# A decoder layer on one core: the pool branch behind the u products, the samples' attention in steps between gate products, the side work of the feed-forward begun later, operands at multiples of 256 bytes

## The chip, the core and the metric

The kernel runs on one core of a Trainium2 chip. The metric is the device time of one execution in microseconds. The core has five engines with an instruction queue each: PE (TensorE, matmuls; its weight loads are listed as PEld), DVE (VectorE), ACT (ScalarE), POOL (GpSimd) and SP (SyncE, which issues all DMAs here). Each engine works its queue in order, and semaphores make it wait for the others.

## The reference, cut to what matters

One layer of a decoder, for a prompt of 2048 tokens and eight samples of four tokens, D_MODEL = 1024. All weights, states and outputs are in float32.

```python
def token_mixer(xn, mem_k, mem_v, pool_prev, n_prev, lp):
    proj = xn @ lp['w_in']          # columns: u, v (512 each) | pool input (256) | queries (256) | 3 gates (1024 each)
    a_part, b_part, q_part, g_part = ...
    u, v = jnp.split(jax.nn.gelu(a_part), 2, axis=-1)
    vn = layernorm(v, lp['gmlp_ln_g'], lp['gmlp_ln_b'])
    sg = chunk_spatial(vn, ...)                      # causal 128x128 mixing within chunks
    br_a = (u * sg) @ lp['w_branch_a']
    pooled = multi_scale_pool(xb_ext, n_prev)        # windows 2, 4, 8, 16; mean minus self
    mixed = einsum('btgd,gde->btge', pooled, lp['w_pool']) * lp['pool_scale']
    br_b = mixed @ lp['w_branch_b']
    br_c = cross_attn(q, mem_k, mem_v) @ lp['w_branch_c']
    gates = sigmoid(g_part + lp['b_gate'])
    merged = gates[0] * br_a + gates[1] * br_b + gates[2] * br_c
    return merged @ lp['w_out'], vn, new_pool

def conv_ffn(hn, conv_prev, lp):                      # D_FF = 2816
    g, u = jnp.split(hn @ lp['w_up'], 2, axis=-1)
    c = lp['conv_b'] + sum(lp['conv_w'][k] * g_ext[:, k:k + T] for k in range(3))
    return (gelu(c) * u) @ lp['w_down'], g_ext[:, -2:]
```

Both parts stand between RMS norms and are added to the residual. The prompt attends to 256 memory tokens whose keys and values are computed here; each sample attends to 256 tokens of its own, read from `cache_mem_k` and `cache_mem_v` (256 KB each a sample).

## The kernel before

Every float32 operand is split in two halves, hi and lo, and a product is the sum of three matmuls (hi hi, hi lo, lo hi). The large products are also taken apart by a scheme with seven block products in place of eight. One block product is `product` (line 392): 4 x 3 = 12 matmuls of 256, 272 or 512 columns. The weights for the scheme are loaded as `raw`, summed on DVE (L363 to L368, tiles `sm`), and split by ACT (L113, hi) and DVE (L114, lo) into tiles `u`.

The tokens are worked in four blocks of 512. Block 1 also holds the 32 rows of the samples (`smp`, 544 columns, products of 272). In each block `mixer` runs, in program order: the v products and their gelu; the pool pair and the q pair (seven products of 12 matmuls for each, of 256 columns); the memory attention; the u products; the spatial mixing (L818 on); 12 gate pairs (`jp` 0 to 3, three each) with the branch products between them; and the output projection with `mg`. Around this stand:

- `norm_v` (L641 to L651), the layer norm of v on DVE with its root on POOL, directly behind the pool pair; then the window sums of the pool branch, `pool_mean` (L575 to L595, tiles `E`, `s`, `po`), and the matmuls with `w_pool` (L729, tiles `wpb` and `po`), behind the q pair.
- in block 0, `stage_consts`, which loads the small inputs (`vl`, `stc`, `wsn`, `wbn`) and transposes them on PE (L474, L483, L500, L514), called inside the v products.
- in block 1, `sample_attn` (L939 on): the cached keys and values of eight samples come through two buffers (`kb`), one DMA each (L950, L973), with transposes (L954), scores (L957), a softmax, and values (L977). It runs as one piece ahead of the gate pairs.
- side work for the feed-forward, `pair_steps`, a generator called the builder here: it loads (`fx<-hd`), scales (POOL, L247), transposes (PE, L231) and sums columns of the normed residual into further operands. Its items are worked in blocks 1 to 3 and in the first half of the up products, `up(0)`, at the places where `next(steps)` stands.

`up(0)` works prompt tokens with products of 512 columns, `up(1)` the rest and the samples with 272 and 256; the results go to memory as `acts`. The down products read them back (`load_acts`, tiles `a`, L136 to L138 with 512 columns).

The code gives the program order; the framework's scheduler then puts each engine's instructions in an order by its own estimates, so the order of rows on an engine is not that of the code. Tiles are placed in SBUF by pools, whose sizes decide the start addresses: `brA`, `brB` and `mg` have halves of 544 x 4 = 2176 bytes, `a` has halves of 1056 x 4 = 4224 bytes (both an odd multiple of 128).

## Time and profile before

| | |
|---|---|
| median of 3 runs | 2800.13 us (2793.3 to 2800.8) |
| profiled execution | 2799.83 us, of which the span of the trace is 2798.1 us |
| mean granted TensorE clock | 0.987 |
| block 0 (v, pool, q, memory, u, gates, output) | from 10 to about 385 us |
| block 1 with the samples | to about 750 us |
| blocks 2 and 3 | to 1371 us |
| up(0), up(1) | to 1834 and 2265 us |
| down | to the end |

In the windows, the column PEclk is the granted clock as a share of full speed, 2.4 GHz; 0.50 is the other level, 1.2 GHz. A matmul's duration in the timeline includes its way through the array, so back-to-back matmuls overlap: what one costs is the distance from start to start.

### The profile page before, as it was taken

How to read it: one execution, taken by the hardware profiler on the slowest of the kernel's cores; microseconds unless marked ns; L12 is line 12 of the kernel's file. 1: busy time of each engine (PE TensorE's matmuls, PEld its weight loads, DVE VectorE, ACT ScalarE, POOL GpSimd, SP SyncE). 2: the span in 40 equal slices, each digit the busy share in tenths (PEclk: the TensorE clock that was granted, in tenths of full speed). 3: DMA queues.
4: the chain of work that ended last, by engine and by line, in shares of the span. 5: the costliest groups of instructions: out<-in, count | busy, mean ns of one | idle time of the engine just before them, and what ended most of it. 6: DMA issues, size and time to landing. Idle time of an engine off the chain costs nothing.

```text
span 2798.1 us, 45245 instructions
## 1 busy us (share of the span) xinstructions
PE 2711.8 (97%) x16833; PEld 2408.8 (86%) x16833; DVE 2059.0 (74%) x3915; ACT 1261.8 (45%) x2377; POOL 247.9 (9%) x321
## 2 busy tenths in 40 slices
PE   6899999999999999999899999999999999999998
PEld 5799878899889988999778788889999998888887
DVE  7688858478587777877587777767777767768665
ACT  4565546455566565755444433433333343215112
POOL 2022020111002101110101100000000000001001
PEclk9899999999999999999999999999999999999999
DMA  5467634476646674577743522442222245326212
GB/s 196 143 215 235 232 114 138 154 225 200 196 131 210 209 263 133 168 232 225 255 138 116 150 90 83 141 174 85 61 85 84 63 151 176 100 75 207 94 67 93
DMA packets 434927, 427.32 MB, mean 153 GB/s; under 512 B 28182, under 2 KB 365611, under 8 KB 432651
## 3 DMA queue, kind: packets, MB, share of 16 engines
q1 hardware_dynamic: 434706, 424.42, 47.4%
q8 instruction: 133, 2.18, 0.3%
q14 instruction: 88, 0.71, 0.1%
HBM read 328.29 MB, written 96.15 MB: 152 GB/s over the span
## 4 chain that ended last, share of the span: by engine, by line
PE 39%; issue 9%; POOL 1%; DVE 1%; DMA 0%; ACT 0%; SPq 0%; POOLq 0%; DVEq 0%; ACTq 0%
PE mm L392 30%; PE mm L138 3%; PE mm L137 3%; PE mm L136 3%; POOL rs L143 0%; POOL rs L145 0%; PE tp L231 0%; POOL fx L247 0%; DVE Y L1160 0%; DVE X L303 0%; DVE Y L193 0%; DMA fx<-hd 0%; DMA xd<-fx 0%; ACT tp L158 0%; DVE u L114 0%
## 5 line engine op out<-in xcount | busy, mean ns | idle before, releaser
L113 ACT CAST u<-raw 128x512 fp32r<-128x512 f32 x884 | 539.3, 621 | 993.7 <-PE mm L392 387.2
L392 PE MATMUL mm<-X,u 128*128 128x512 f32 (+2 forms) x5544 | 896.0, 322 | 8.2 <-ACT t L410 3.6
L392 PEld LDWEIGHTS mm<-X,u 128*128 128x128 f32 x5544 | 801.0, 189 | 95.6 <-DVE t L451 4.5
L114 DVE TENSOR_TENSOR u<-raw,u 128x512 fp32r<-128x512 f32 x884 | 600.4, 689 | 198.9 <-ACT u L113 189.9
L392 PE MATMUL mm<-xs,u 128*128 128x256 f32 (+1 forms) x4608 | 619.7, 291 | 16.7 <-ACT t L410 6.1
L392 PEld LDWEIGHTS mm<-xs,u 128*128 128x128 f32 x4608 | 583.5, 193 | 36.8 <-ACT u L113 7.9
L1160 DVE TENSOR_TENSOR Y<-Y,mm 128x512 f32<-128x512 f32 x268 | 182.8, 685 | 110.6 <-PE mm L138 109.8
L138 PE MATMUL mm<-u,a 128*128 128x512 f32 x616 | 244.6, 397 | 0.0
L137 PE MATMUL mm<-u,a 128*128 128x512 f32 x616 | 243.5, 395 | 0.0
L136 PE MATMUL mm<-u,a 128*128 128x512 f32 x616 | 241.5, 392 | 0.0
L143 POOL TENSOR_SCALAR rs<-ss 128x1 f32<-128x1 f32 (+2 forms) x57 | 31.3, 550 | 1520.3 <-ACT tp L158 1519.7
L136 PEld LDWEIGHTS mm<-u,a 128*128 128x128 f32 x616 | 117.0, 190 | 26.6
L137 PEld LDWEIGHTS mm<-u,a 128*128 128x128 f32 x616 | 115.7, 188 | 27.0
L138 PEld LDWEIGHTS mm<-u,a 128*128 128x128 f32 x616 | 115.7, 188 | 25.6
L1084 DVE SCALAR_TENSOR_TENSOR d<-gE,vecs,d 128x1024 f32<-128x1024 f32 x88 | 112.5, 1278 | 6.1 <-ACT d L1082 5.6
L113 ACT CAST u<-sm 128x512 fp32r<-128x512 f32 x120 | 74.4, 620 | 88.1 <-PE mm L392 66.3
L247 POOL TENSOR_SCALAR fx<-fx,rt 128x256 f32<-128x256 f32 x64 | 74.4, 1171 | 421.3 <-DMA fx<-hd 266.1
L114 DVE TENSOR_TENSOR u<-sm,u 128x512 fp32r<-128x512 f32 x120 | 82.5, 688 | 39.6 <-ACT u L113 38.8
L392 PE MATMUL mm<-xa,u 128*128 128x256 f32 x768 | 108.8, 293 | 1.8 <-DVE u L114 1.6
L392 PEld LDWEIGHTS mm<-xa,u 128*128 128x128 f32 x768 | 99.3, 197 | 5.7 <-DVE u L114 2.7
L420 DVE TENSOR_TENSOR t<-mm,t 128x256 f32<-128x256 f32 (+2 forms) x130 | 60.9, 468 | 56.7 <-PE mm L392 56.2
L136 PE MATMUL mm<-u,mg 128*128 128x512 f32 x224 | 88.7, 396 | 0.0
(302 smaller groups left out, 3848.8 us busy)
## 6 DMA issues: line engine op xcount, KB each, us to landing
raw<-in_w_in SPq DMA_DIRECT2D x96, 512.0 KB
raw<-ws SPq DMA_DIRECT2D x96, 512.0 KB
raw<-in_w_up SPq DMA_DIRECT2D x88, 512.0 KB
raw<-in_w_down SPq DMA_DIRECT2D x44, 512.0 KB
raw<-in_w_out SPq DMA_DIRECT2D x32, 512.0 KB
md<-fx SPq DMA_DIRECT2D x24, 512.0 KB
raw<-in_w_in SPq DMA_DIRECT2D x48, 256.0 KB
act<-d SPq DMA_DIRECT2D x22, 528.0 KB
```

What stands on the lines that cost most here:

```text
L113: S.copy(uv[:, 0], src)
L114: V.tensor_tensor(uv[:, 1], src, uv[:, 0].bitcast(F32), ALU.subtract)
L136: T.matmul(ps, lhsT=lh, rhs=wh, start=first, stop=False)
L137: T.matmul(ps, lhsT=lh, rhs=wl, start=False, stop=False)
L138: T.matmul(ps, lhsT=ll, rhs=wh, start=False, stop=last)
L143: G.tensor_scalar(r[:n], ms, more, EPS, ALU.add, ALU.add)
L247: G.tensor_scalar(part, part, r, None, ALU.mult)
L392: T.matmul(ps, lhsT=u[:, wl, k], rhs=x(k, xl)[:, c0:c0 + n], start=not more and k + i == 0, stop=k + i == 5, skip_group_check=True)
L420: V.tensor_tensor(v7, pc, v, ALU.add)
L1084: V.scalar_tensor_tensor(d[j][:, 0:FSB], gE[j][:, k:k + FSB], cw(k, f), d[j][:, 0:FSB], ALU.mult, ALU.add)
L1160: return V.tensor_tensor(yd, yd, ps, ALU.add)
```

## The change

The core of the diff:

```diff
+AC = 1088
...
     def up_pools():
         upool["smtag"] = "sm"
+        pad = uctx.enter_context(tc.tile_pool(name="pad", bufs=1, side="right"))
+        G.memset(pad.tile([P, 56], F32, name="pad"), 0.0)
...
-            if b == 0:
-                stage_consts()
+            if b == 1:
+                stage_conv()
...
-            brB = [hb([P, 2, 2, NTB], name="brB") for _ in range(2)]
+            brB = [hb([P, 2, 2, n_all], name="brB") for _ in range(2)]
...
-            norm_v()
+            if b == 0:
+                stage_consts()
             for i in range(2):
                 E = Ep[i]
...
             for _ in att:
                 pass
+            norm_v()
+            for i, po in enumerate(pooled):
+                for (c0, n) in subs:
+                    ps = tp()
+                    T.matmul(ps[:, :n], lhsT=C["wpb"][:, i], rhs=po[:, c0:c0 + n], start=True, stop=True)
...
-            if smp:
-                sample_attn(sw, brB[1])
+            satt = sample_attn(sw, brB[1]) if smp else iter(())
...
-                    next(steps, None)
+                    if not smp or jp:
+                        next(steps, None)
                     gt = [w2.tile([P, NTB], F32, name="gt", tag="w2") for _ in range(2)]
-                    for h, j, *it in pair(1536 + i * D + jp * 256):
+                    for h, j, *it in pair(1536 + i * D + jp * 256, satt):
...
-                mg.append(hb([P, 2, 2, NTB], name="mg"))
+                mg.append(hb([P, 2, 2, n_all], name="mg"))
...
+            for b in range(2):
+                DMA.dma_start(kbs[b], ck[b])
+            yield
+            for b in range(8):
+                if b:
+                    score(b - 1)
...
+                V.tensor_copy(kbT, t)
+                DMA.dma_start(kbs[b % 2], ck[b + 2] if b < 6 else cv[b - 6])
+                yield
...
-            ahead = {1: ffn_items(0)[:4], 2: ffn_items(0)[4:], 3: ffn_items(1) + ffn_items(2)[:4]}
+            ahead = {1: ffn_items(0)[:2], 2: ffn_items(0)[2:6], 3: ffn_items(0)[6:] + ffn_items(1) + ffn_items(2)[:2]}
...
-                for _ in range(2):
+                for _ in range(2 if q else 0):
                     next(steps, None)
...
-        up(0, pair_steps(ffn_items(2)[4:] + ffn_items(3), vecs[:, 114:122], fx), first["X"], first["W"])
+        up(0, pair_steps(ffn_items(2)[2:] + ffn_items(3), vecs[:, 114:122], fx), first["X"], first["W"])
...
-                t = hb([P, 2, FSB + NS], name="a")
+                t = hb([P, 2, AC], name="a")
```

`stage_conv` is the part of `stage_consts` that loads and transposes `state_conv` (`stc`), cut out of it. `brA` gets `n_all` as `brB` does. `sample_attn` is a generator now: it takes a step after each block product of the three gate pairs of `jp` 0 (21 products), loads each cache piece two steps ahead, and the values' loads are begun while keys are still worked. The last transposes of the pool state (`sc`, `npp`) move behind the q pair. The halves of `a` become 1088 x 4 = 4352 bytes, those of `brA`, `brB` and `mg` (outside block 1) 2048 bytes, and `pad` moves the pools on the right side by 224 bytes, among them a tile of operands of the up products; all of these then start at multiples of 256 bytes. The number of matmuls stays.

What the scheduler made of it is shown at three places. The first is PE in block 0, from the end of the pool pair to the q pair; `xa`, `xs` are token operands, and 12 rows of L392 (in the changed file L395) are one block product. Before:

```order
L392 MATMUL mm<-xs,u 128x256 x12
L392 MATMUL mm<-xa,u 128x256 x2
L392 MATMUL mm<-xs,u 128x256 x12
L729 MATMUL tp<-po,wpb 128x512
L392 MATMUL mm<-xa,u 128x256 x10
L729 MATMUL tp<-po,wpb 128x512
L392 MATMUL mm<-xs,u 128x256 x12
L392 MATMUL mm<-xa,u 128x256 x36
```

and now:

```order
L395 MATMUL mm<-xs,u 128x256 x12
L490 MATMUL tp<-ident,vl 128x122
L508 MATMUL tp<-ident,wsn 128x128 x4
L395 MATMUL mm<-xa,u 128x256 x4
L395 MATMUL mm<-xs,u 128x256 x12
L395 MATMUL mm<-xa,u 128x256 x5
L522 MATMUL tp<-ident,wbn 32x32 x4
L395 MATMUL mm<-xa,u 128x256 x3
L395 MATMUL mm<-xs,u 128x256 x2
L395 MATMUL mm<-xa,u 128x256 x4
L395 MATMUL mm<-xs,u 128x256 x10
L395 MATMUL mm<-xa,u 128x256 x32
```

The two L729 matmuls have left the q pair, and the transposes of `vl`, `wsn` and `wbn` (L490, L508, L522), which stood inside and behind the v products, stand in it. On DVE the sums and splits for q's second product still stand behind the window sums of the pool branch, but the first part of those sums, q's first split and `norm_v`'s last instruction are no longer between the last L684 and them; the copies of the transposes stand ahead of the last L684.

The second is PE in block 1 in the samples' attention. Before, in its second half of keys:

```order
L392 MATMUL mm<-xs,u 128x272 x8
L957 MATMUL tp<-kb_5274,sw 128x256 x2
L954 MATMUL tp<-ident,kb_5273 128x128 x8
L392 MATMUL mm<-xs,u 128x272 x2
L957 MATMUL tp<-kb_5274,sw 128x256 x4
L954 MATMUL tp<-ident,kb_5273 128x128 x8
L957 MATMUL tp<-kb_5274,sw 128x256 x4
L954 MATMUL tp<-ident,kb_5273 128x128 x4
L957 MATMUL tp<-kb_5274,sw 128x256 x2
L968 MATMUL tp<-ident,kb_5274 128x128 x2
L977 MATMUL tp<-kb_5274,kb_5273 128x8 x12
L392 MATMUL mm<-xs,u 128x272 x6
```

and now:

```order
L963 MATMUL tp<-kb_5322,sw 128x256 x2
L976 MATMUL tp<-ident,kb_5321 128x128 x4
L395 MATMUL mm<-xs,u 128x272 x12
L963 MATMUL tp<-kb_5322,sw 128x256 x2
L976 MATMUL tp<-ident,kb_5321 128x128 x4
L395 MATMUL mm<-xs,u 128x272 x12
L963 MATMUL tp<-kb_5322,sw 128x256 x2
L976 MATMUL tp<-ident,kb_5321 128x128 x4
L395 MATMUL mm<-xs,u 128x272 x12
L963 MATMUL tp<-kb_5322,sw 128x256 x2
L976 MATMUL tp<-ident,kb_5321 128x128 x4
L395 MATMUL mm<-xs,u 128x272 x12
```

Where eight, two or no gate matmuls stood between one sample's work and the next, there are now 12.

The third is PE at the start of `up(0)` and DVE beside it. PE before, from the end of the output projection:

```order
L392 MATMUL mm<-X,u 128x512 x77
L231 MATMUL tp<-ident,fx 128x128 x4
L392 MATMUL mm<-X,u 128x512 x3
L231 MATMUL tp<-ident,fx 128x128 x2
L392 MATMUL mm<-X,u 128x512
L231 MATMUL tp<-ident,fx 128x128 x2
L392 MATMUL mm<-X,u 128x512 x75
```

PE now, with tile numbers, from the 55th matmul of `up(0)` on (156 of them stand ahead of the first L232):

```order
L395 MATMUL mm_15672<-X_15460,u_15429 128x512 x6
L395 MATMUL mm_15686<-X_15462,u_15432 128x512 x6
L395 MATMUL mm_15686<-X_15466,u_15432 128x512 x6
L395 MATMUL mm_15755<-X_15438,u_15728 128x512 x6
L395 MATMUL mm_15755<-X_15440,u_15728 128x512 x6
L395 MATMUL mm_15686<-X_15470,u_15435 128x512 x6
L395 MATMUL mm_15769<-X_15442,u_15734 128x512 x6
```

DVE now, at the same place (L933 and L934 finish the output of block 3, rows group by rows group; L304 makes the lo half of an operand `X`):

```order
L933 SCALAR_TENSOR_TENSOR mix_15120<-mix_15120,rs2_15502,post_row_660 128x512 x2
L934 TENSOR_TENSOR mix_15120<-mix_15120,xr_15498 128x512 x2
L417 TENSOR_TENSOR t1_15615<-mm_15631,t1_15615 128x512
L115 TENSOR_TENSOR u_15728<-raw_15723,u_15728 128x512
L933 SCALAR_TENSOR_TENSOR mix_15121<-mix_15121,rs2_15522,post_row_660 128x512 x2
L934 TENSOR_TENSOR mix_15121<-mix_15121,xr_15518 128x512 x2
L423 TENSOR_TENSOR t2_15616<-mm_15658,t1_15615 128x512
L115 TENSOR_TENSOR u_15734<-sm_15727,u_15734 128x512
L933 SCALAR_TENSOR_TENSOR mix_15121<-mix_15121,rs2_15542,post_row_660 128x512 x2
L934 TENSOR_TENSOR mix_15121<-mix_15121,xr_15538 128x512 x2
L304 TENSOR_TENSOR X_15470<-X_15470 128x1024
```

The transposes of the builder (L231, now L232) have gone from the first 77 matmuls to behind 156. The seventh block product, with `u_15435` and `X_15470`, is the first that reads a lo half made behind the last L934.

## Rows read from the trace of the kernel before

**Rows 1.** Page, part 1: busy us (share of the span) and instructions per engine.

```profile
PE 2711.8 (97%) x16833; PEld 2408.8 (86%) x16833; DVE 2059.0 (74%) x3915; ACT 1261.8 (45%) x2377; POOL 247.9 (9%) x321
```

**Rows 2.** Windows of the stages; the first line names the columns.

```profile
core 0: us, PE busy (x) PEld busy (x) DVE busy (x) ACT busy (x) POOL busy (x), PEclk, DMA share, GB/s
23.90:34.10 10.20, 7.37 (x22) 5.24 (x20) 8.61 (x25) 5.04 (x12) 1.98 (x1) 0.67 0.63 188
47.50:90.10 42.60, 32.48 (x198) 27.35 (x194) 37.08 (x74) 13.57 (x31) 7.95 (x10) 0.84 0.39 136
64.80:78.50 13.70, 10.28 (x35) 7.98 (x36) 11.18 (x23) 3.68 (x7) 0.00 (x0) 0.50 0.57 188
406.40:436.80 30.40, 27.00 (x184) 24.95 (x182) 28.89 (x71) 12.63 (x31) 6.43 (x6) 0.94 0.29 90
480.00:526.60 46.60, 40.35 (x241) 36.19 (x240) 17.81 (x35) 15.96 (x36) 3.28 (x8) 0.85 0.51 167
505.20:518.70 13.50, 12.57 (x58) 12.48 (x59) 2.49 (x7) 4.70 (x15) 1.72 (x4) 0.50 0.34 118
774.60:797.80 23.20, 17.33 (x102) 14.60 (x101) 21.81 (x42) 7.01 (x16) 4.92 (x10) 0.85 0.27 79
1085.00:1106.00 21.00, 17.42 (x130) 15.68 (x130) 20.75 (x42) 7.25 (x13) 3.06 (x6) 1.00 0.31 101
1384.00:1430.00 46.00, 38.52 (x160) 30.32 (x161) 37.11 (x71) 22.65 (x43) 11.15 (x16) 0.93 0.53 168
```

**Rows 3.** PE's waits over the span: total us, times, longest us.

```profile
PE tp L729 <- DVE po L595: 7.7, 2, 5.3
```

**Rows 4.** Timeline, block 0's pool and q products: start us, us, engine.

```profile
55.72 1.30 SPq L100 DMA_DIRECT2D raw<-in_w_mem_kv  x2
...
58.81 1.69 PE L392 MATMUL mm<-xs,u 128*128 128x256 f32 x12 [0.28 <-DVE E L684]
...
60.73 0.42 DVE L684 TENSOR_TENSOR E<-mm,t 128x256 f32<-128x256 f32 x1
...
62.75 1.41 DVE L591 SCALAR_TENSOR_TENSOR po<-s,E 64x512 f32<-64x512 f32 x2
...
72.51 0.69 DVE L114 TENSOR_TENSOR u<-sm,u 128x512 fp32r<-128x512 f32 x1 [0.26 <-ACT u L113]
...
73.45 3.55 PE L392 MATMUL mm<-xs,u 128*128 128x256 f32 x12
```

**Rows 5.** Timeline, sample attention: last key load and its first reader.

```profile
495.64 0.37 SPq L950 DMA_DIRECT2D kb<-in_cache_mem_k  x1
...
499.72 0.52 PE L954 MATMUL tp<-ident,kb 128*128 128x128 f32 x3 [0.29 <-DMA kb<-in_cache_mem_k]
```

**Rows 6.** Timeline, start of the up products.

```profile
1377.94 2.10 POOL L247 TENSOR_SCALAR fx<-fx,rt 128x256 f32<-128x256 f32 x2 [7.12 <-DMA fx<-hd]
...
1382.03 1.41 DVE L922 SCALAR_TENSOR_TENSOR mix<-mix,rs,post_row 128x512 f32<-128x512 f32 x2 [3.69 <-POOL rs L145]
...
1395.67 1.22 DVE L303 TENSOR_TENSOR X<-X 128x1024 fp32r<-128x1024 f32 x1
...
1399.98 18.67 PE L392 MATMUL mm<-X,u 128*128 128x512 f32 x75
```

**Rows 7.** PE timeline, 512-column products, two stretches without idle time.

```profile
373.34 0.39 PE L136 MATMUL mm<-u,xs 128*128 128x512 f32 x1
...
377.19 0.39 PE L138 MATMUL mm<-u,xs 128*128 128x512 f32 x1
...
2359.67 0.40 PE L138 MATMUL mm<-u,a 128*128 128x512 f32 x1
...
2364.34 0.40 PE L137 MATMUL mm<-u,a 128*128 128x512 f32 x1
```

**Rows 8.** PE's matmuls by line and shape: count, busy us, mean ns.

```profile
L136 PE MATMUL mm<-u,a 128*128 128x512 f32 x616 | 241.5, 392 | 0.0
...
L136 PE MATMUL mm<-u,mg 128*128 128x512 f32 x224 | 88.7, 396 | 0.0
```

More of the change, by code (lines that the diff above doesn't have):

```diff
@@ L464, in decoder_step, with stage_conv @@
         C = {}
+        def stage_conv():
+            st = A["state_conv"].rearrange("l b j (f p) -> (l b j f) p", p=P)
+            sl_ = w4.tile([P, D], F32, name="stc", tag="w4")
+            t = tp()
+            for i, (r0, rn) in enumerate(((0, 128), (128, 128), (256, 96))):
+                DMA.dma_start(sl_[:rn, i * P:(i + 1) * P], st[r0:r0 + rn])
+                T.transpose(t[:, r0:r0 + rn], sl_[:rn, i * P:(i + 1) * P], ident[:rn, :rn])
+            V.tensor_copy(scT.rearrange("p r f -> p (r f)"), t[:, 0:352])
+        hal = mc.tile([P, 2, PSTATE], F32, name="hal")
+        G.memset(hal, 0.0)
+        C["hal"] = hal
         def stage_consts():
@@ L476, in stage_consts @@
             V.tensor_scalar(vb, t[:, 0:24], 0.5, None, ALU.mult)
-            st = A["state_conv"].rearrange("l b j (f p) -> (l b j f) p", p=P)
-            sl_ = w4.tile([P, D], F32, name="stc", tag="w4")
-            t = tp()
-            for i, (r0, rn) in enumerate(((0, 128), (128, 128), (256, 96))):
-                DMA.dma_start(sl_[:rn, i * P:(i + 1) * P], st[r0:r0 + rn])
-                T.transpose(t[:, r0:r0 + rn], sl_[:rn, i * P:(i + 1) * P], ident[:rn, :rn])
-            V.tensor_copy(scT.rearrange("p r f -> p (r f)"), t[:, 0:352])
             lng = row_bcast(mc, A["gmlp_ln_g"], "lng")
@@ L725, in mixer @@
             qT = [(qq[:, 0, i], qq[:, 1, i]) for i in range(2)]
-            for i, po in enumerate(pooled):
-                for (c0, n) in subs:
-                    ps = tp()
-                    T.matmul(ps[:, :n], lhsT=C["wpb"][:, i], rhs=po[:, c0:c0 + n], start=True, stop=True)
-                    hi = brB[0][:, 0, i, c0:c0 + n]
-                    S.activation(hi, ps[:, :n], AF.Copy, scale=vecs[:, 112 + i:113 + i])
-                    V.scalar_tensor_tensor(brB[0][:, 1, i, c0:c0 + n], ps[:, :n], vecs[:, 112 + i:113 + i],
-                                           hi.bitcast(F32), ALU.mult, ALU.subtract)
+            for i in range(2):
+                if smp:
+                    t = tp()
+                    sc = w2.tile([P, NTB], F32, name="sc", tag="w2")
+                    V.tensor_copy(win3(sc[:, 0:NS], 8), Es3[i][:, :, 15:19])
+                    T.transpose(t[:NS, 0:P], sc[:, 0:NS], ident)
+                    V.tensor_copy(nps[:NS, i * P:(i + 1) * P], t[:NS, 0:P])
+                if b == NB - 1:
+                    t = tp()
+                    T.transpose(t[:PSTATE, 0:P], Ep[i][:, TB:TB + PSTATE], ident)
+                    V.tensor_copy(npp[:PSTATE, i * P:(i + 1) * P], t[:PSTATE, 0:P])
+            if smp:
+                for bb in range(8):
+                    DMA.dma_start(O["new_pool_sample"][0, bb, 11:15], nps[4 * bb:4 * bb + 4, 0:BW])
+            if b == NB - 1:
+                DMA.dma_start(O["new_pool_prompt"][0, 0], npp[:PSTATE, 0:BW])
             if b == 0:
@@ L800, in mixer @@
             next(att)
-            brA = [hb([P, 2, 2, NTB], name="brA") for _ in range(2)]
+            brA = [hb([P, 2, 2, n_all], name="brA") for _ in range(2)]
             us = []
@@ L851, in mixer @@
                         gates[i, j] = gt[j]
+                for _ in satt:
+                    pass
                 for jj in range(2):
@@ L959, in sample_attn @@
                              start=b + hp == 0, stop=b == 7 and hp == 1)
+            for b in range(2):
[4 more added lines that the diff above has]
+                    score(b - 1)
+                t = tp()
+                for hp in range(2):
+                    for mt in range(2):
+                        T.transpose(t[:, hp * M + mt * P:hp * M + (mt + 1) * P], kbs[b % 2][:, mt, hp * P:(hp + 1) * P],
+                                    ident)
+                V.tensor_copy(kbT, t)
+                DMA.dma_start(kbs[b % 2], ck[b + 2] if b < 6 else cv[b - 6])
+                yield
+            score(7)
             nm = stat.tile([P, 1], F32, name="nm1", tag="nm1")
@@ L965, in sample_attn @@
             V.tensor_scalar(pr, pr, sm, None, ALU.mult)
+            for _ in range(3):
+                yield
             t = tp()
@@ L969, in sample_attn @@
             V.tensor_copy(pT, t[:, 0:M])
+            yield
             ao = tp()
             for b in range(8):
[L972 to L973 removed]
                 for hp in range(2):
@@ L1092, in up @@
                     S.activation(d[j][:, 0:n_all], d[j][:, 0:n_all], AF.Gelu_apprx_tanh, bias=vecs[:, 90 + f:91 + f])
-                next(steps, None)
+                if q:
+                    next(steps, None)
                 W = right_factors(w_up, DFF + c)
```

42 lines of the change are left out of this document (12 added, 30 removed).

## The prediction

> **What bounds the kernel now.** I began with the page's busy times [rows 1]: PE works 2711.8 of 2798.1 us (97%), the next engine, DVE, 74%. PE is the bound, and no part of the change takes a matmul away, so there are three places where time can come from: PE's idle time (86 us), the stretches in which PE works at the lower clock, and the distance between matmuls that follow each other without a wait. The DVE and ACT times count only where PE waits for them.
>
> For the first two I asked for the windows of the stages that the change touches [rows 2]. Busy time times the granted clock is the work at full clock; the window's length less that is what the stage loses. This is an estimate, since the clock is a mean over the window. It gives: consts in the v products (23.9 to 34.1) 10.2 - 7.37 x 0.67 = 5.3 us; block 0's pool and q (47.5 to 90.1) 42.6 - 32.48 x 0.84 = 15.3; block 1's 30.4 - 27.0 x 0.94 = 5.0; sample attention 46.6 - 40.35 x 0.85 = 12.3; block 2's pool and q 23.2 - 17.33 x 0.85 = 8.5; block 3's 21.0 - 17.42 = 3.6; the start of the up products (1384 to 1430) 46.0 - 38.52 x 0.93 = 10.2. Together 60 us: that is all that moving work about can give back here. A third of it is clock: in block 0 and in the sample attention the level falls to 1.2 GHz behind PE's idle time and stays there for 13.7 and 13.5 us, while PE is busy for 10.28 and 12.57 us [rows 2].
>
> **Part by part.** The profiled execution took 2799.83 us (span 2798.1), the median of the runs is 2800.13; I reckon from 2799.8.
>
> *Consts out of the v products.* PE no longer stops there for `vl` and `stc`; the 5.3 us go, less about 0.6 for three transposes that now stand in block 1. Gain 5 (4 to 5.3).
>
> *Block 0, pool and q.* PE waits 7.7 us for `po` at L729 [rows 3]. But with L729 gone, q's second product still needs a split that stands behind the window sums on DVE, in the new order too. Before, DVE came from the last L684 (60.73) to that split's end (72.51 + 0.69 = 73.2), and PE went on at 73.45 [rows 4]: it waited for this split as much as for `po`. The new order takes from this chain the first L591 pair (1.41 [rows 4]) and three more instructions (one of `norm_v`, a window sum, a split) of about the split's 0.69, 3.5 us in all, and puts copies ahead of it. Against it stand the loads of `vl`: they are issued behind the first load of `in_w_mem_kv`, which went out at 55.72 (1.30 us for two issues [rows 4]), and PE comes to their transposes at about 58.2, ahead of the product that began at 58.81 [rows 4]. At up to 0.65 us an issue the last of the five is out by 59.6 at the latest; the one landing in these rows is the key load's, 4.1 us after issue [rows 5], and these pieces are far smaller. I take a stop of 2 us (0 to 5), and it delays the last L684 by as much. What is left of 3.5 is near 1; the clock and the earlier start of q add to it. I take 3, between 0 (the late consts eat it) and 8 (no lower clock).
>
> *Block 1, pool and q.* The stops are short ones on L684, splits and copies that stood behind `norm_v`; of 5.0 I take 4 (2 to 5).
>
> *Sample attention in steps.* The 12.3 us are the round trips PE, DVE, PE with nothing between. Now a block product of 12 matmuls, 1.69 us in the row for 256 columns [rows 4], hides the copy and the transposes of each step. What remains is the loads: the last key load went out at 495.64 and its reader started at 499.72 after a wait for it [rows 5], 4.1 us, while the value phase gives a buffer two block products, about 3.4 us. That is up to 0.7 us for each of six loads, 4 in all. I take a gain of 9.5 (5 to 12). The 13 builder steps left in block 1 hide under the other gate pairs.
>
> *Blocks 2 and 3, pool and q.* In block 2 q's splits no longer stand between `po` and PE, and nothing PE needs stands behind `norm_v`: 7 of 8.5 (4 to 8). In block 3 the wait is the one at the pool state's transposes, which now stand behind the q pair: 3 of 3.6 (2 to 3.6). `norm_v` and the sums are late next at the spatial mixing; the u products lie between, tens of us of PE work, and DVE has a quarter of its time free [rows 1].
>
> *Builder later.* At the start of `up(0)` POOL worked two L247 (2.10 us from 1377.94) ahead of the roots for the second group of output rows, and DVE's L922 came at 1382.03 [rows 6]. Without them that is up to 1.8 us earlier, and the last `X` half, made on DVE behind the fourth group at 1395.67 to 1396.89 [rows 6], comes at about 1395.1. In the new order PE has 84 matmuls of 0.227 us, 19 us, from 1371 on, with a short stop by 1391, and then needs this half: a new stop of about 4 us. Before, PE ran freely only from 1399.98 on [rows 6], with 81 matmuls and eight small transposes done. The gain is then about 4.9 here and some 1.6 in later transposes that wait no more: 6.5 (2 to 10).
>
> *Addresses.* The stretch from 373.34 to 377.19 has 17 starts of L136 to L138 with operand `xs`, 226.5 ns each; that from 2359.67 to 2364.34 has 20 starts of the same three lines with `a`, 233.5 ns each; both without idle time, with the same 128x512 shape and at full clock [rows 7]. Worked from the tiles' placement, the operands of the first start at multiples of 256 bytes, while one half of `a` lies 128 bytes beside one. So I take it that a start beside the grid costs between 5 and 7 ns. The change moves to the grid the 1848 matmuls with `a` (three lines of 616) and 624 of the 672 with `mg` (three of 224, less block 1's 48) [rows 8], by the same count in the code 576 with `brA` and `brB` outside block 1, and some 150 with the tile behind `pad`: 3200 in all. At 5.2 ns that is 16.6 us; the bounds are 0 (the operand, not its address, makes the difference) and 3200 x 7 = 22.
>
> The sum: 5 + 3 + 4 + 9.5 + 7 + 3 + 6.5 + 16.6 = 54.6, so 2745 us. All low ends together give 19, or 2781; all high ends 74, or 2726.
>
> **The rivals.** *Addresses do nothing.* For it: both stretches of [rows 7] differ in the operand as well as in its address, and one is in the mixer, the other in the down products. Then 16.6 us are missing: 2761. The Trainium skill, page "SBUF — State Buffer", section "Operand start alignment", asks only for a start at a multiple of the element size, 4 bytes for float32, and adds that this is "about legality, not speed", with nothing timed. By that rule, read as a rule on time, all operands of before were aligned already, and this rival would hold. The trace speaks against it so far, with 226.5 and 233.5 ns.
>
> *The stops move.* DVE is busy for 37.08 of 42.6 us in block 0's stage, 21.81 of 23.2 in block 2's and 20.75 of 21.0 in block 3's [rows 2]: if DVE is the bound of these stages, PE stops at the next split or `E` instead, and the lower clock comes back. Then the terms of blocks 0, 1, 2 and 3 and of the up products (23.5 together) shrink to a third: 2761.
>
> *Late cache pieces.* In block 1 the SP queue is in order, and 16 loads that wait for their buffers stand among the weight loads. If a weight load is held for 2 us at six of these places, PE loses 12 us, and sample attention gains nothing: about 2755.
>
> *Slower.* The shift of the pools puts other operands of the up and down products in worse places: a conflict between operands that now start alike would show in matmuls that run at 227 ns now. It decides from (38 + 8.4) us over 16833 matmuls, 2.8 ns each: above that the kernel is slower than before, at 5 ns about 2846. Against it: operands on the grid are the quickest in the trace.
>
> **How the numbers follow.** The forecast's own case has 0.52 (range 2726 to 2757). Addresses that do nothing have 0.16, stops that move 0.18, late pieces 0.08, slower 0.03; 0.03 is left for all low ends falling together. A difference under 0.3% (8.4 us) can't be told from none here; only that last case and the edge of the second rival come near it. So faster 0.93, same 0.04, slower 0.03. The range is 2715 to 2775: it takes in the first three rivals, and below it some us for stops that I did not count.
>
> **What the profile after would show.** Addresses: L136 to L138 with `a` and `mg` start 227 ns apart, and the down products take 9 us less. Consts: no half clock at 27 us, a stop of about 2 us at L490. Block 0: a stop of some 7 us ahead of q's second product. Block 1: L963 and L1000 with waits under 1 us, clock 1.00 in the window. Block 2: no half clock. Up: a stop of about 4 us behind the 84th matmul. The prediction is wrong if the `a` matmuls stay above 231 ns, if the half clock returns in blocks 0 to 2 at the old length, or if the matmuls with `X` run slower than before.

## The result and the profile after

The changed kernel takes 2749.6 us (median of 4 runs, 2747.5 to 2751.0) against 2800.3 us for the kernel before: ratio 0.9824 [0.9807, 0.9841]. The forecast was 2745, the range 2715 to 2775. The profiled execution took 2749.03 us (before 2799.83), so it has 50.8 us to explain. In the changed file the lines are numbered a little higher: L136 to L138 are now L137 to L139, L392 is L395, L113 and L114 are L114 and L115, L684 is L690.

The page's busy times answer to [rows 1]: the same number of matmuls, PE busy for 35.8 us less.

```profile
PE 2676.0 (97%) x16833; PEld 2394.2 (87%) x16833; DVE 2057.3 (75%) x3915; ACT 1261.6 (46%) x2377; POOL 253.6 (9%) x322
```

The windows of the same stages answer to [rows 2]; the columns are those named there. The stages stand earlier now, and some windows are longer than before, so what is to be compared is the loss: length less busy time times clock.

```profile
23.90:34.10 10.20, 6.78 (x24) 5.22 (x23) 8.91 (x23) 5.48 (x14) 0.00 (x0) 0.83 0.68 206
44.00:87.00 43.00, 36.62 (x224) 30.19 (x223) 36.96 (x76) 13.24 (x31) 6.99 (x15) 0.92 0.43 137
398.00:426.00 28.00, 26.50 (x193) 25.16 (x192) 26.76 (x68) 13.08 (x32) 3.86 (x4) 0.94 0.30 95
466.00:500.00 34.00, 33.03 (x240) 30.98 (x240) 23.67 (x47) 14.60 (x28) 0.00 (x0) 1.00 0.44 136
744.00:770.00 26.00, 23.82 (x185) 22.32 (x185) 23.12 (x43) 13.75 (x32) 2.87 (x6) 1.00 0.43 130
1050.00:1073.00 23.00, 19.98 (x147) 19.14 (x148) 21.76 (x46) 9.09 (x17) 2.27 (x4) 0.93 0.39 127
1340.00:1410.00 70.00, 64.64 (x279) 52.45 (x277) 59.68 (x101) 34.88 (x61) 15.13 (x20) 0.95 0.42 130
```

Worked out as in the prediction, the losses are now 4.6 us (consts' place in the v products; 5.3 before), 9.3 (block 0's pool and q; 15.3), 3.1 (block 1's; 5.0), 1.0 (sample attention; 12.3), 2.2 (block 2's; 8.5), 4.4 (block 3's; 3.6) and 8.6 (start of the up products; 10.2). So the attention gave nearly all it had and block 2 three quarters of it; the first and the last gave little, and block 3's loss is 0.8 higher than before.

PE's waits over the whole span say what stands in the old places. The columns are as in [rows 3], and the 7.7 us for `po` there have no row any more.

```profile
PE mm L395 <- ACT u L114: 9.5, 5, 5.0
...
PE mm L395 <- DVE gE L1105: 5.1, 1, 5.1
PE tp L232 <- POOL fx L248: 4.9, 5, 1.9
...
PE mm L395 <- DVE E L690: 3.6, 2, 3.0
PE mm L138 <- DVE u L115: 3.4, 1, 3.4
```

The longest stops of the places that the change touches have their rows on PE's timeline (start us, us, engine, and in brackets the idle time and what ended it). The first is in the v products, the next two in block 0's q pair, then the attention, block 3 and the up products:

```profile
29.29 0.80 PE L138 MATMUL mm<-u,xa 128*128 128x512 f32 x1 [3.42 <-DVE u L115]
...
54.78 0.27 PE L490 MATMUL tp<-ident,vl 122*128 122x122 f32 x1
...
64.17 0.80 PE L395 MATMUL mm<-xs,u 128*128 128x256 f32 x2 [5.02 <-ACT u L114]
...
486.65 0.63 PE L976 MATMUL tp<-ident,kb 128*128 128x128 f32 x4 [0.95 <-DMA kb<-in_cache_mem_k]
...
1059.69 4.56 PE L395 MATMUL mm<-xs,u 128*128 128x256 f32 x24 [3.02 <-DVE E L690]
...
1359.23 5.13 PE L395 MATMUL mm<-X,u 128*128 128x512 f32 x13 [5.12 <-DVE gE L1105]
```

The transposes of `vl` at 54.78 waited for nothing. In the up products DVE makes the half of `X` that the prediction named, and behind it `gE`, for which PE waited to the end:

```profile
1357.10 1.22 DVE L304 TENSOR_TENSOR X<-X 128x1024 fp32r<-128x1024 f32 x1
...
1358.41 1.27 DVE L1105 TENSOR_TENSOR gE<-mm,t 128x512 f32<-128x512 f32 x2
```

The stop of 5.02 us ends with a split on ACT for q's second product. What is split there, `sm`, is made on DVE by L366 to L368. The timeline of DVE and ACT has these between the window sums (L589 to L594), and ACT's split behind the last of them:

```profile
58.26 0.42 DVE L690 TENSOR_TENSOR E<-mm,t 128x256 f32<-128x256 f32 x1
...
60.29 0.69 DVE L366 TENSOR_TENSOR sm<-raw 128x512 f32<-128x512 f32 x1
...
61.51 0.69 DVE L367 TENSOR_TENSOR raw<-raw 128x512 f32<-128x512 f32 x1
62.11 0.70 DVE L593 TENSOR_TENSOR s<-s 128x520 f32<-128x520 f32 x1
62.72 0.68 DVE L368 TENSOR_TENSOR sm<-raw 128x512 f32<-128x512 f32 x1
...
63.49 0.62 ACT L114 CAST u<-sm 128x512 fp32r<-128x512 f32 x1 [3.89 <-DVE sm L368]
...
65.68 0.68 DVE L115 TENSOR_TENSOR u<-sm,u 128x512 fp32r<-128x512 f32 x1
```

Down products, against the second stretch of [rows 7]: 20 starts of the same three lines from 2318.07 to 2322.60, 226.5 ns each; before it was 233.5. Over all starts with `a` that follow another within 260 ns, the means are 227.0 and 232.1 ns.

```profile
2318.07 0.39 PE L138 MATMUL mm<-u,a 128*128 128x512 f32 x1
...
2322.60 0.39 PE L137 MATMUL mm<-u,a 128*128 128x512 f32 x1
```

The whole by place, as the distance from one first matmul to the next on PE's timeline (the first with `brA`, `mg`, `X`, `a` of each stage), in us:

| stage | before | after | change | forecast without addresses |
|---|---|---|---|---|
| start of the trace to block 0's first `brA` | 180.2 | 171.2 | -8.9 | -8 (consts 5, pool and q 3) |
| block 0's output, block 1 to its first `brA` | 214.8 | 195.5 | -19.3 | -13.5 (pool 4, attention 9.5) |
| block 1's output, block 2 to `brA` | 176.7 | 170.3 | -6.5 | -7 |
| block 2's output, block 3 to `brA` | 163.7 | 163.1 | -0.6 | -3 |
| first to last 512-column matmul of `up(0)` | 449.8 | 446.7 | -3.2 | -6.5 |
| first `a` to the last one | 503.1 | 493.5 | -9.6 | 0 (addresses 1848 x 5.2 ns = 9.6) |
| all other stages (gates, output of block 3, rest of up) | 1101.1 | 1098.3 | -2.8 | 0 (addresses, with the other stages, 7) |

### The profile page after: what moved, and what is told of

Read it like the earlier page. It is cut to its first block, busy times and chain, and to the rows that moved or that the text cites. A ratio compares the mean times of both kernels' runs of the same rounds, so it can differ in the third digit from the quotient of the medians.

```text
span 2747.3 us, 45219 instructions
## 1 busy us (share of the span) xinstructions
PE 2676.0 (97%) x16833; PEld 2394.2 (87%) x16833; DVE 2057.3 (75%) x3915; ACT 1261.6 (46%) x2377; POOL 253.6 (9%) x322
## 4 chain that ended last, share of the span: by engine, by line
PE 74%; issue 11%; DVE 6%; DMA 4%; ACT 3%; POOL 2%; SPq 0%; DVEq 0%; POOLq 0%; ACTq 0%
PE mm L395 49%; PE mm L137 5%; PE mm L139 5%; PE mm L138 5%; PE mm L132 2%; PE mm L134 2%; PE mm L133 2%; DVE u L115 1%; POOL rs L144 1%; ACT tp L159 1%; PE tp L232 1%; POOL rs L146 1%; DMA raw<-ws 1%; PE tp L780 1%; PE tp L745 1%
## 5 line engine op out<-in xcount | busy, mean ns | idle before, releaser
L114 ACT CAST u<-raw 128x512 fp32r<-128x512 f32 x884 | 540.0, 621 | 984.1 <-PE mm L395 379.7
L395 PE MATMUL mm<-X,u 128*128 128x512 f32 (+2 forms) x5544 | 892.5, 322 | 11.3 <-DVE gE L1105 5.1
L395 PEld LDWEIGHTS mm<-X,u 128*128 128x128 f32 x5544 | 797.9, 188 | 97.3 <-ACT t L413 6.2
L115 DVE TENSOR_TENSOR u<-raw,u 128x512 fp32r<-128x512 f32 x884 | 600.7, 688 | 190.8 <-ACT u L114 180.2
L395 PE MATMUL mm<-xs,u 128*128 128x256 f32 (+1 forms) x4608 | 612.1, 290 | 20.1 <-ACT u L114 6.3
L395 PEld LDWEIGHTS mm<-xs,u 128*128 128x128 f32 x4608 | 578.8, 192 | 36.1 <-DVE gt L626 10.8
L137 PE MATMUL mm<-u,a 128*128 128x512 f32 x616 | 240.5, 390 | 0.0
L139 PE MATMUL mm<-u,a 128*128 128x512 f32 x616 | 240.1, 390 | 0.0
L138 PE MATMUL mm<-u,a 128*128 128x512 f32 x616 | 239.9, 389 | 0.0
L139 PEld LDWEIGHTS mm<-u,a 128*128 128x128 f32 x616 | 115.7, 188 | 24.1
L137 PEld LDWEIGHTS mm<-u,a 128*128 128x128 f32 x616 | 115.7, 188 | 23.7
L138 PEld LDWEIGHTS mm<-u,a 128*128 128x128 f32 x616 | 115.7, 188 | 23.6
L248 POOL TENSOR_SCALAR fx<-fx,rt 128x256 f32<-128x256 f32 x64 | 81.2, 1278 | 426.6 <-DMA fx<-hd 240.7
L115 DVE TENSOR_TENSOR u<-sm,u 128x512 fp32r<-128x512 f32 x120 | 82.6, 689 | 40.9 <-ACT u L114 40.2
L114 ACT CAST u<-sm 128x512 fp32r<-128x512 f32 x120 | 74.6, 621 | 84.0 <-PE mm L395 65.1
L395 PE MATMUL mm<-xa,u 128*128 128x256 f32 x768 | 106.4, 289 | 1.8 <-ACT u L114 1.0
L395 PEld LDWEIGHTS mm<-xa,u 128*128 128x128 f32 x768 | 97.9, 194 | 4.1 <-ACT u L114 1.6
L859 ACT ACTIVATE gt<-gt,vb 128x512 f32<-128x512 f32 (+1 forms) x96 | 70.1, 730 | 39.4 <-DVE gt L626 38.5
```

The source lines that it names most:

```text
L114: S.copy(uv[:, 0], src)
L115: V.tensor_tensor(uv[:, 1], src, uv[:, 0].bitcast(F32), ALU.subtract)
L137: T.matmul(ps, lhsT=lh, rhs=wh, start=first, stop=False)
L138: T.matmul(ps, lhsT=lh, rhs=wl, start=False, stop=False)
L139: T.matmul(ps, lhsT=ll, rhs=wh, start=False, stop=last)
L248: G.tensor_scalar(part, part, r, None, ALU.mult)
```

## Experiments

The theory is the prediction's sum: each part pays at its own place, and the addresses pay by the place of the operands and not by their kind. The rivals are its first two, addresses that do nothing and stops that only move, and a third that came with the result: parts that pay only together. In the tables and below, "against the changed kernel" is against 2749.6.

**The addresses alone, and all but the addresses.** `e1_align_only` is the kernel before with this edit, `e2_no_align` the changed kernel without it:

```diff
+AC = 1088
...
+        pad = uctx.enter_context(tc.tile_pool(name="pad", bufs=1, side="right"))
+        G.memset(pad.tile([P, 56], F32, name="pad"), 0.0)
...
-            brB = [hb([P, 2, 2, NTB], name="brB") for _ in range(2)]
+            brB = [hb([P, 2, 2, n_all], name="brB") for _ in range(2)]
...
-                    t = hb([P, 2, FSB + NS], name="a")
+                    t = hb([P, 2, AC], name="a")
```

(and the same for `brA`, `mg` and the tile `ar`).

> The kernel before with the addresses alone changed (halves of a, brA, brB and mg, and the pad). If a start beside a multiple of 256 bytes costs 5 to 7 ns in every 512-column matmul and PE has no slack to lose it in: 3200 x 5.2 = 16.6 us less, 2784 us, down products 9.6 us shorter. If it costs this only where nothing else bounds PE, and the gate stages wait for other engines anyway: about 10 to 12 less (the a products and those with X), 2789. If the address does nothing and the operand makes the difference: 2800.

> The changed kernel with the addresses of before. Address theory: 2749.6 + 16.6 = 2766, with L137 to L139 on a back at 232 ns from start to start. Half of it if only the down products count: 2760. Address does nothing: 2750.

Measured: e1 2782.4 us, ratio 0.9939 [0.9927, 0.9951], 18.5 us less than before; e2 2768.6 us, 0.9884 [0.9872, 0.9897], 19 more than the changed kernel. From the first `a` to the last, e1 takes the 493.5 us of the changed kernel, e2 the 503.1 of the kernel before. Both ways agree, and nothing else was edited: the addresses are worth 18.5 to 19 us, 9.6 of them in the down products.

**Halves 64 bytes off.** `e7_ac1072` is the changed kernel with halves of `a` of 1072 x 4 = 4288 bytes, 64 bytes short of a multiple of 256, so that the lo halves and some tiles behind them are off the grid (multiples of 256):

```diff
-AC = 1088
+AC = 1072
```

> The changed kernel with the halves of a at 1072 x 4 = 4288 bytes: the lo half starts 192 bytes beside a multiple of 256, and some u tiles of the down products 64 beside one. If the grid is 256 bytes: those matmuls at 230 to 233 ns from start to start, the others at 227, the down products 5 to 7 us longer, 2755 to 2757. If a multiple of 64 is enough: all at 227, 2750.

Measured: 2762.0 us, 0.9862 [0.9849, 0.9876], 12.3 more than the changed kernel. The timeline of the down products has 20 starts from 2334.08 to 2338.70, 231 ns each, and the stretch from the first `a` to the last is 9.4 us longer, nearly the whole gain.

```profile
2334.08 0.39 PE L139 MATMUL mm<-u,a 128*128 128x512 f32 x1
...
2338.70 0.39 PE L138 MATMUL mm<-u,a 128*128 128x512 f32 x1
```

One size was changed by 64 bytes, the operand is the same, and the distance follows (the mean over all starts with `a` is 231.6 ns). So it is the place of the operands: with halves of 4224 bytes, a multiple of 128, and of 4288, a multiple of 64, the matmuls are slow, with 4352, a multiple of 256 and not of 512, they are quick. The execution profiled is the slowest of the four (2767.4), 18.4 us above the profile of the changed kernel. Beside the 9.4, 5.2 of them lie in block 0 and 1.9 in the second half of the up products, where nothing was edited and profiles differ by such amounts.

**The samples' attention alone.** `e3_attn_only` is the kernel before with `sample_attn` as a generator and nothing more:

```diff
-            if smp:
-                sample_attn(sw, brB[1])
+            satt = sample_attn(sw, brB[1]) if smp else iter(())
...
-                    next(steps, None)
+                    if not smp or jp:
+                        next(steps, None)
...
-                    for h, j, *it in pair(1536 + i * D + jp * 256):
+                    for h, j, *it in pair(1536 + i * D + jp * 256, satt):
```

> The kernel before with the samples' attention in steps alone (and no builder step in the three gate pairs of jp 0 in block 1). As predicted: 9.5 us less, 2791, with waits for the cache pieces of up to 0.7 us each. If the loads hide too, as the trace of the changed kernel has it (one wait of 0.95 us): 13 to 14 less, 2787. If late pieces eat it: 2800.

Measured: 2789.3 us, 0.9961 [0.9949, 0.9972], 11.6 us less than before. At its place the edit is worth more: block 1's stage is 14.8 us shorter, but block 2's is 4.5 us longer. PE's waits from 690 to 790 us have two rows that the kernel before does not have there:

```profile
PE tp L231 <- POOL fx L247: 1.8, 2, 1.6
PE mm L136 <- DVE mixF L912: 1.4, 1, 1.4
```

The three step places that the attention takes from the builder are missing: eight of the 48 transposes with `fx` that belong to block 1, two items, now stand behind the first matmul with `mg`, where in the kernel before there is none. The changed kernel gives block 1 two items in place of four.

**The items of each block.** `e12_items_back` puts four items into block 1 again, in the changed kernel:

```diff
-            ahead = {1: ffn_items(0)[:2], 2: ffn_items(0)[2:6], 3: ffn_items(0)[6:] + ffn_items(1) + ffn_items(2)[:2]}
+            ahead = {1: ffn_items(0)[:4], 2: ffn_items(0)[4:], 3: ffn_items(1) + ffn_items(2)[:4]}
...
-        up(0, pair_steps(ffn_items(2)[2:] + ffn_items(3), vecs[:, 114:122], fx), first["X"], first["W"])
+        up(0, pair_steps(ffn_items(2)[4:] + ffn_items(3), vecs[:, 114:122], fx), first["X"], first["W"])
```

> The changed kernel with the builder's items per block as before, still begun with the second pair of up products. If the late start alone carries the gain of 15.7: 2750. If the items carry it (four items in the shorter rest of block 1 are worked off in a heap): 2756 to 2765. Half and half: about 2757.

Measured: 2756.9 us, 0.9842 [0.9829, 0.9856], 7.3 more than the changed kernel. The two intervals overlap, the times do not (2754.8 to 2759.2 against 2747.5 to 2751.0), and the loss has its place: the stage of block 1's output and block 2 is 6.7 us longer. The wait at the output projection is there again, as in e3:

```profile
PE mm L137 <- DVE mixF L921: 2.1, 1, 2.1
```

So moving items is no gain of its own. It keeps what the attention in steps would otherwise give back.

**The builder, alone and undone.** `e11_builder_only` is the kernel before with both edits of the builder, `e6_builder_back` the changed kernel with both undone; beside the items above they are:

```diff
-                for _ in range(2):
+                for _ in range(2 if q else 0):
                     next(steps, None)
...
-                next(steps, None)
+                if q:
+                    next(steps, None)
```

> The kernel before with the builder alone begun later and its items moved. Prediction's term: 6.5 less, 2794. If it is worth what undoing it in the changed kernel cost (15.7): 2785. If it is worth what the up products gained between the two traces (3 to 4): 2797.

> The changed kernel with the builder's items and steps of before (steps in the first pair of up products, four items in block 1). Prediction's term: 6.5 slower, 2756. From the stages of the two traces: 3.5 slower, 2753. Builder's place doesn't matter: 2750.

Measured: e11 2798.5 us, 0.9994 [0.9985, 1.0003], no difference; e6 2765.3 us, 0.9871 [0.9857, 0.9884], 15.7 more than the changed kernel, of which e12 accounts for 7.3. In e11 the waits of PE from 1340 to 1600 are led by a new one:

```profile
PE mm L392 <- DVE gE L1079: 5.1, 1, 5.1
```

In e6 they are the old ones, and its window from 1334 to 1600 has PE busy for 251.43 us at a clock of 0.97:

```profile
PE tp L232 <- POOL fx L248: 10.8, 7, 2.4
PE mm L395 <- ACT t L413: 3.7, 1, 3.7
```

```profile
1334.00:1600.00 266.00, 251.43 (x1094) 203.03 (x1093) 203.98 (x365) 120.04 (x208) 38.39 (x40) 0.97 0.46 137
```

The changed kernel in the same window:

```profile
1334.00:1600.00 266.00, 256.32 (x1139) 207.77 (x1138) 212.86 (x379) 121.66 (x211) 40.70 (x41) 0.99 0.45 136
```

The loss is 266 - 251.43 x 0.97 = 22.1 us in e6 and 12.2 in the changed kernel; e6 comes to the up products 9 us later, but from the first to the last 512-column matmul of `up(0)` it is 9.9 us longer too. The late start is worth some 8 us in the changed kernel (e6 less e12) and about 1 in the kernel before (e11, with the items). e11 and the changed kernel have the same new stop of 5.1 us; e6's old waits come to 14.5 us, against 12.3 in the kernel before (8.7 for `fx`, 3.6 for `t`, same view). That difference is 2 us of the 7; why the early start costs the rest more there stays open.

**The pool branch, with and without the consts.** `e4_pool_only` is the kernel before with the pool part and `norm_v` moved, the consts where they were; `e5_pool_consts` has the consts moved as well:

```diff
-            norm_v()
...
+            norm_v()
+            for i, po in enumerate(pooled):
+                for (c0, n) in subs:
...
```

and in e5 also

```diff
-            if b == 0:
-                stage_consts()
+            if b == 1:
+                stage_conv()
...
+            if b == 0:
+                stage_consts()
             for i in range(2):
```

> The kernel before with the pool branch and the norm of v behind the u products; the consts stay in the v products. If the consts' waits in the v products cost 5 us of their own (the prediction's term): 5 us slower than the run with both moves. If they only covered a later wait of the v products for a split on DVE (the changed kernel has a stop of 3.4 us there): within 2 us of the run with both.

> The kernel before with the pool branch and the norm of v behind the u products, and the consts moved. Sum of the predicted terms: 5 + 3 + 4 + 7 + 3 = 22 less, 2778. From the two traces by stage: 9 (block 0), 5 (block 1), 6.5 (block 2), 0.6 (block 3), 21 less, 2779. If DVE is the bound and the stops move: 7 less, 2793.

Measured: e4 2783.5 us, 0.9937 [0.9925, 0.9950], 17.8 less than the kernel before beside it (2801.3); e5 2788.9 us, 0.9954 [0.9939, 0.9970], 11.9 less. The intervals overlap; the windows show the difference more plainly. Those of e4, then those of e5:

```profile
23.90:34.10 10.20, 7.64 (x22) 5.50 (x21) 7.98 (x23) 4.41 (x10) 1.87 (x1) 0.67 0.64 185
44.00:87.00 43.00, 37.16 (x227) 28.95 (x226) 39.66 (x80) 14.04 (x32) 7.82 (x12) 1.00 0.43 149
```

```profile
23.90:34.10 10.20, 6.42 (x18) 5.11 (x19) 8.81 (x21) 3.87 (x9) 0.00 (x0) 0.67 0.67 196
44.00:87.00 43.00, 36.70 (x221) 30.35 (x221) 35.78 (x74) 12.31 (x29) 7.26 (x15) 0.88 0.42 137
```

The losses are 5.1 and 5.8 us in e4, 5.9 and 10.7 in e5. Without the consts in block 0 the stops at q's second product are 1.48 us and less, and the clock stays at 1.00. With them there is one of 5.02 us. And in the v products, from which the consts were taken, PE now stops in one piece, for a split. The first row is from there, the second from the q pair:

```profile
27.68 0.80 PE L137 MATMUL mm<-u,xa 128*128 128x512 f32 x1 [3.93 <-DVE u L114]
...
63.57 0.80 PE L392 MATMUL mm<-xs,u 128*128 128x256 f32 x2 [5.02 <-ACT u L113]
```

With the consts in place PE waits there three times for `vl` and `stc` (0.85, 1.17 and 0.54 us in e4), and goes on with the same matmul as soon as the same split is made. DVE and PE in the kernel before, then DVE in the changed one, whose PE goes on at 29.29:

```profile
28.11 3.69 DVE L114 TENSOR_TENSOR u<-raw,u 128x512 fp32r<-128x512 f32 x6
...
28.84 0.80 PE L137 MATMUL mm<-u,xa 128*128 128x512 f32 x1
```

```profile
28.55 3.69 DVE L115 TENSOR_TENSOR u<-raw,u 128x512 fp32r<-128x512 f32 x6
```

The matmul starts 0.73 and 0.74 us behind the start of the first of these six splits, 0.75 in e4 and 0.77 in e5. So the consts' waits had covered a wait for the split, and the trace of the kernel before has it already. In the stages behind, e4 and e5 have the whole of block 2's gain (6.2 and 6.8 us) and 5.0 and 3.1 us in block 1's.

**The consts put back, in the changed kernel.** `e10_consts_back`:

```diff
-            if b == 1:
-                stage_conv()
+            if b == 0:
+                stage_consts()
             vn = hb([P, 4, AW], F32, name="vn")
...
-            if b == 0:
-                stage_consts()
             for i in range(2):
                 E = Ep[i]
```

> The changed kernel with the consts back in the v products. If moving them costs, because their transposes and copies stand between the E sums and q's splits on DVE (5.2 us of stop there with them, stops of 1 to 2 us without): some 5 us less than the changed kernel, 2744 to 2745, faster than both kernels. If the move gives what the prediction said (5 us in the v products): 2755.

Measured: 2753.1 us (2748.1 to 2756.3), 0.9827 [0.9813, 0.9841]; the changed kernel has 0.9824. The move of the consts is worth nothing that can be told, either way. Its windows lose 5.2 and 6.5 us; those of the changed kernel 4.6 and 9.3. What block 0 gains without them, some 3 us, doesn't reach the end in the median.

**The next stop in block 0.** Two attempts to remove the 5.02 us. `e9_q_first` writes the sums and splits for q ahead of the window sums; `e13_no_sums` leaves the window sums of block 0 out (a copy of `E` takes the place of `po`):

```diff
+            W_q = weights(2 * AW + BW) if b == 0 else None
             if b == 0:
                 stage_consts()
...
-            for h, j, *it in pair(2 * AW + BW):
+            for h, j, *it in pair(2 * AW + BW, None, W_q):
```

```diff
+            if first:
+                V.tensor_copy(out, E[:, :, 15:L])
+                return
             Tn = L - PSTATE
```

> The changed kernel with block 0's sums and splits for the q pair ahead of the window sums of the pool branch. If the stop of 5.0 us ahead of q's second product and the half clock behind it are DVE's window sums standing ahead of these splits: the stop goes, 5 to 8 us less, 2742 to 2745. If another wait takes its place (the consts' loads, the last E): 2750.

> The changed kernel without block 0's window sums (the pool branch of block 0 is a copy of its input, part of the computation is left out), which takes some 7 us of work from DVE ahead of q's splits. If DVE's work is the bound of block 0's pool and q stage: the stop of 5.2 us ahead of q's second product and the half clock behind it go, 6 to 8 us less, 2742 to 2744. If the wait that is next (the memory's norm, then the scores at L745 with 2.6 us) takes it up: 2748 to 2750.

Measured: e9 2754.0 us, 0.9827 [0.9813, 0.9840]; e13 2749.3 us, 0.9814 [0.9800, 0.9827]. Neither is faster than the changed kernel. In e9 the stop is gone from q and has become one of 6.38 us for the norm of the memory tokens (`xt`, L542), which DVE now comes to later:

```profile
73.12 0.87 PE L547 MATMUL tp<-ident,xt 128*128 128x128 f32 x3 [6.38 <-DVE xt L542]
```

In e13 the stop at q is 1.22 us, and the first `brA` comes 3.9 us sooner. The profile gives 2.9 of them back in `up(0)`, where nothing was edited: from 1440 to 1480 the clock is 0.96 in e13 and 1.00 in the changed kernel. One profile of each does not show that the one causes the other.

What each version changes at the places, in us against the kernel before, from the same first matmuls as the table of the result:

| version | to block 0's `brA` | block 1 | block 2 | block 3 | `up(0)` | `a` |
|---|---|---|---|---|---|---|
| changed kernel | -8.9 | -19.3 | -6.5 | -0.6 | -3.2 | -9.6 |
| e1, addresses alone | -2.2 | -0.5 | 0.0 | 0.1 | -0.9 | -9.6 |
| e2, no addresses | -9.9 | -18.3 | -6.4 | 0.2 | -1.5 | 0.0 |
| e3, attention alone | -2.6 | -14.8 | +4.5 | 0.9 | 1.5 | 0.0 |
| e4, pool alone | -8.6 | -5.0 | -6.2 | 0.1 | 1.6 | 0.0 |
| e5, pool and consts | -8.2 | -3.1 | -6.8 | 0.2 | 3.5 | 0.0 |
| e6, builder undone | -7.9 | -19.1 | -3.0 | -0.5 | +6.7 | -9.5 |
| e12, items undone | -8.8 | -19.0 | +0.3 | -0.6 | -3.1 | -9.6 |

e1 and e3 edit nothing ahead of block 0's first `brA` but a start address, and still differ there by 2 to 3 us; a figure of that size in one profile is not evidence. Block 0 can be read from more than one profile, since PE's instructions stand in the same order there in the kernel before, e1, e3 and e11, and again in the changed kernel, e2, e6, e7 and e12 (e1 and e2 with other start addresses). The first `brA` comes at 177.5 to 180.2 us in the four (mean 178.3) and at 170.2 to 173.9 in the five (171.8). The first `mg`, at the end of the block, comes at 325.5 to 327.4 (326.5) and at 319.7 to 325.5 (322.1). So block 0 gains some 6.5 us up to `brA` and some 4.4 in all; the 8.9 of the one pair of profiles is near the upper end.

## Why the prediction was right, step by step

**Addresses, 16.6: right, a little low.** 18.5 alone, 19 undone. The down products gain the 9.6 us that 1848 x 5.2 ns gives; the other 9 were put at 7. The prediction doesn't say where its 5.2 comes from: the two stretches that it shows give 7.0, and 1848 x 7.0 would have been 12.9. The means over all starts with `a`, 232.1 and 227.0, give 5.1. The rival that addresses do nothing falls. By the rule that it took from the Trainium skill (page "SBUF — State Buffer", section "Operand start alignment": aligned to the element is aligned), read as a rule on time, e1 would have been equal to the kernel before. The measurement decides: 18.5 us. The section itself says that it is not about speed.

**Sample attention, 9.5: right, too low.** 14.8 us in block 1's stage when done alone, 11.6 at the end. The 14.8 are more than the 12.3 that its window had lost, so the loss reckoned from busy time was no upper bound. The term that was mis-sized is the loads: 2.8 us were deducted for six waits of up to 0.7 us, and one of 0.95 us came, at L976. The 4.1 us from issue to first reader [rows 5] were too dear as a steady price: the six loads of the value phase (issued from 503.11 to 514.39) were read 3.6 to 5.0 us after their issue, and PE waited for none. With the rest of the stage's stops gone too, the window loses 1.0 of 12.3 us and the clock stays at 1.00.

**Block 1's pool, 4, and block 2's, 7: right.** 5.0 and 6.2 us in e4, where they stand alone. Block 2's window shows 1.00, as forecast.

**Consts, 5: wrong.** The step that failed is "PE no longer stops there". PE stops there for 3.42 us, for a split that was late on DVE and hidden by the consts' waits; the stage loses 4.6 us where it lost 5.3. Nor is the half clock gone: it stands from 28.7 to 32.1. In the kernel before it lasted twice as long there, but in e1, with the old order, 3.4 us as well, so the 0.7 us less can't be put down to the move. The forecast stop of 2 us at `vl` did not come either, since `vl`'s loads went out some 7 us sooner than reckoned: the first load of `in_w_mem_kv`, which they follow, was issued at 48.29 in place of 55.72. SP's timeline:

```profile
48.29 0.38 SPq L101 DMA_DIRECT2D raw<-in_w_mem_kv  x1
...
50.27 0.27 SPq L488 DMA_DIRECT2D vl<-in_norm_ffn_pre  x1
```

**Block 0, 3: too low, for the same reason.** The window loses 6.0 us less. From the last `E` to the end of the first split's lo half DVE takes 65.68 + 0.68 - 58.26 = 8.1 us, before 12.5 [rows 4]; 3.5 had been taken off, 4.4 came off, and no stop at `vl` was to be paid. (One copy of the transposes, L523 with 0.28 us, stands behind the last `E` and not ahead of it.) This and the consts are two errors that cancel: 8 forecast up to the first `brA`, 8.9 in the pair of profiles and 6.5 in the means of all with the same order. That the sum fits there is luck. The stop ahead of q's second product that the prediction expected (some 7 us) is there with 5.02.

**Block 3, 3: wrong.** The rival "the stops move" holds here. PE stops 3.02 us for `E`, which stands on DVE behind the last of `norm_v` and two splits. That nothing PE needs stands behind `norm_v`, as the prediction has it for block 2, does not hold in block 3: in the code `norm_v` follows the q pair, but in the scheduler's order its instructions are ahead:

```profile
1056.94 0.74 DVE L655 SCALAR_TENSOR_TENSOR vn<-vn,rs,lnb 128x512 f32<-128x512 f32 x1
1057.60 0.68 DVE L115 TENSOR_TENSOR u<-raw,u 128x512 fp32r<-128x512 f32 x1
1058.20 0.42 DVE L690 TENSOR_TENSOR E<-mm,t 128x256 f32<-128x256 f32 x1
1058.54 0.68 DVE L115 TENSOR_TENSOR u<-raw,u 128x512 fp32r<-128x512 f32 x1
...
1059.21 0.42 DVE L690 TENSOR_TENSOR E<-mm,t 128x256 f32<-128x256 f32 x1
```

**Builder, 6.5: the stop was right, the price was not.** The new stop stands where it was forecast, behind the 84th matmul, 5.1 us for 4. The half of `X` that the prediction named was done at 1357.10 + 1.22 = 1358.32, which would have been a stop of 4.2; what ended it was `gE`, which stands behind that half on DVE and was not in the prediction. The edit alone brings 1 us, within what can't be told (e11); 3.2 us are seen in `up(0)` of the changed kernel. Yet undoing it costs 15.7 (e6), nearly as much as undoing the addresses. The term had no place for that: it priced the edit against the kernel before only.

Together: e1, e3, e5 and e11 are worth 18.5 + 11.6 + 11.9 + 1.1 = 43.1 us one by one, the change 50.7. The 7.6 between them is no more than the five intervals allow together (an estimate from them: about 8), and with e4 in place of e5 the sum is 49.0. So the sum doesn't show that the parts pay more together; the builder does, with 1.1 alone and 15.7 undone. e3 with e12 shows one reason, the builder's items at the end of block 1 (4.5 to 7.3 us); the rest is open. Neither the attention nor the pool branch was undone in the changed kernel. That 54.6 was forecast and 50.7 measured is in part luck: the consts and block 3 (8 us) gave nothing that can be told, the builder alone 1 of 6.5, and the addresses and the attention made up for 4 of it.

## What to carry to other kernels

Before taking a wait away, look for the next thing that is late at the same place on the engine that feeds it; here a wait for small loads covered one for a split, and its removal was worth nothing that could be told. The row that shows it is in the trace before: the first matmul behind the wait starts as soon as another engine's work is done. When a step is moved in code that a scheduler reorders, read the queue of the waiting engine's feeder in the new order, in every block. And where a bound engine runs without idle time, compare the distance between starts by operand: some 5 ns over 1848 matmuls (9.6 us) were worth more than any single stop shown here, for an edit of sizes alone.

## What the runs showed of the hardware

512-column matmuls on float32 halves started 226.5 ns apart with their operands at multiples of 256 bytes, and 233.5 ns apart where one half of `a` lay 128 bytes beside one [rows 7]; with the 64 bytes of e7 it was 231 ns in the stretch shown. The cost is not borne by one of the three matmuls of a product alone: in the kernel before, L136, L137 and L138 with `a` start 234.4, 229.8 and 232.2 ns after the matmul ahead of them on average, though only L138 reads the lo half of `a` (in these products the operand that is loaded as weights); in the changed kernel the three have 226.9 to 227.1. How it comes about, no run here shows.

The granted clock falls to 1.2 GHz at PE's stops in the changed kernel too: in windows that begin in the 3.42-us and in the 5.02-us stop it is 0.50, for 3.4 and 6.8 us, where block 0's q pair had 13.7 us of it before [rows 2]. The time at the lower level is not fixed by the order of the instructions: at the same stop, in the same order, it is 10.2 us in e7 (the last window).

```profile
28.70:32.10 3.40, 2.81 (x7) 2.26 (x8) 3.40 (x6) 0.68 (x2) 0.00 (x0) 0.50 0.44 128
...
62.90:69.70 6.80, 5.12 (x21) 4.79 (x22) 6.57 (x13) 3.62 (x9) 1.21 (x2) 0.50 0.38 152
```

```profile
62.20:72.40 10.20, 6.64 (x28) 6.31 (x29) 9.97 (x19) 4.69 (x11) 1.21 (x2) 0.50 0.54 184
```

Up to 330 us, the profiles that have block 0 in the changed kernel's order spend between 13.6 us (e12) and 30.6 us (e6, e7) at the lower level. This goes with the spread of block 0's end, 319.7 us in e12 and 324.1 and 325.5 in e6 and e7.
